# A sublayer's end: one feature quarter for all tokens, three quarters tile by tile

## The chip, the cores and the metric

The kernel runs on one core of one Trainium2 chip. The metric is the device time of one execution in microseconds; lower is better. The kernel before takes 3494.22 us, the median of three runs (3493.36 to 3494.25).

## The reference

One inference step of a small diffusion transformer: four layers, model width 1024, 128 context tokens and 512 latent tokens, all in 32-bit floats. Layer i mixes tokens by differential attention, neighbourhood attention, grouped-query attention or a long convolution ("hyena"), each followed by a squared-ReLU MLP of width 4096. Around each of the eight sublayers stands the same frame (xp is the context, xs the latent tokens):

```python
hp = modulate(xp, mod_p[0], mod_p[1])              # x * (1 + scale) + shift
...                                                # the mixer: op, os_ = ... @ w_o
xp = layer_norm(DN_ALPHA * xp + mod_p[2] * op, ln_g[i, 0], ln_b[i, 0])
xs = layer_norm(DN_ALPHA * xs + mod_s[2] * os_, ln_g[i, 0], ln_b[i, 0])
fp = squared_relu_mlp(modulate(xp, mod_p[3], mod_p[4]), mlp_w1[i], mlp_w2[i])
fs = squared_relu_mlp(modulate(xs, mod_s[3], mod_s[4]), mlp_w1[i], mlp_w2[i])
xp = layer_norm(DN_ALPHA * xp + mod_p[5] * fp, ln_g[i, 1], ln_b[i, 1])
xs = layer_norm(DN_ALPHA * xs + mod_s[5] * fs, ln_g[i, 1], ln_b[i, 1])
```

So a sublayer ends with a product (512 of the inner features at a time, here the last 512), its gated addition to the residual, a layer norm over the 1024 features of each token, and the modulation that begins the next sublayer.

## The kernel before

The 640 tokens are five tiles of 128 (`NT = 5`); tile 0 is the context. The residual `r` has tokens on the partitions. The input of a stage, `h`, has features on the partitions, since TensorE contracts over them. Every product is made of three (`mm3`, lines 473 to 475): each 32-bit operand is split into a rounded part and a rest (`hh` and `hl` for h, the two halves of a tile `hl...` for weights). A weight comes by DMA into one of three `raw` tiles; ScalarE casts it (line 450) and VectorE subtracts (line 451) into one of five `hl` tiles, in the order in which weights are wanted. `wget(key, ahead)` hands out a weight and has the conversion written for as many weights ahead.

A **group** is one tile's product with one feature **quarter** of 256 (`quarter`): 12 matmuls into one of four small PSUM banks. VectorE multiplies the result by the gate, which empties the bank into a tile `gtmp` (line 653), and the addition to `r` (line 660) is VectorE's if the group is `quick`, otherwise GpSimd's, but for one in four.

`sublayer_end` does the last 20 groups of a sublayer. Quarters 0 and 1 go over all five tiles; as soon as quarter 1 of a tile is added, the statistics of its first 512 features are taken (`ln_half`, line 682). Then, tile by tile, come quarters 2 and 3, both quick, and `ln_norm`: the second statistics, the aggregate, a square root on ScalarE (line 699), two small steps on VectorE, and the normalisation of the 1024 features on ScalarE (line 706; for the last tile half of it on VectorE, line 708).

`ln_out` turns a normalised tile into h: eight transposes on TensorE (line 736) into PSUM, scale and shift by ScalarE for four of the eight blocks (line 742) and by VectorE for the other four (line 745), casts to `hh` on ScalarE (line 746), and the rests into `hl` (line 748), on GpSimd for the first half of tiles 0, 2 and 3, on VectorE otherwise. In the end itself it is done for tiles 0 and 1 behind tile 3, and for tile 2 behind tile 4, with PSUM tiles of two banks of which there are two. Tiles 3 and 4 are left in `pending`: the next stage does its first products for tiles 0 and 1 (256 tokens, 24 matmuls a weight), then calls `flush` for tile 3, does the next weight's, and calls it for tile 4. The next stage's other 384 tokens come after that.

The order on VectorE, ScalarE and SyncE is set by a scheduler when the program is built; on GpSimd it is the written one, and on TensorE too from the `manual_schedule` in `sublayer_end` until the last tile is out. Each engine takes its instructions in that order. After it, `ln_residual` multiplies and shifts the residual by the layer norm's own gain and bias, on GpSimd and VectorE.

Seven of the eight sublayers end so; the last one takes the branch `if last`.

Of the kernel before, what the change touches and what calls it, by code (L numbers as in the profile page):

```python
# [24 lines left out]
NT = TOK // P  # L25
# [5 lines left out]
ALPHA = (2 * DEPTH) ** 0.25  # L31
# [247 lines left out]
class Trunk:  # L279
# [395 lines left out]
        self.hh = self.L(F32R, f"hh{self.tn}").rearrange("p (k t) -> p k t", k=KD)  # L675
        self.hl = self.L(F32R, f"hl_{self.tn}").rearrange("p (k t) -> p k t", k=KD)

    def ln_half(self, t, h, st=None):

        if st is None:  # L680
            st = self.small(12, "st").rearrange("p (a b) -> p a b", a=2)
        self.nc.vector.bn_stats(st[:, h], self.r[:, t, h * 512:(h + 1) * 512])  # L682
        return st

    def ln_norm(self, t, last=False):

        nc = self.nc
        r = self.r[:, t]
        if last:
            st = self.S(F32, "st", 24).rearrange("p (a b) -> p a b", a=4)  # L690
            for h in range(4):
                nc.vector.bn_stats(st[:, h], r[:, h * 256:(h + 1) * 256])
        else:
            st = self.st.pop(t) if t in self.st else self.ln_half(t, 0)
            self.ln_half(t, 1, st)
        mv = self.small(2, "mv")
        nc.vector.bn_aggr(mv, st)
        rs = self.small(2, "rs")
        nc.scalar.activation(rs[:, 0:1], mv[:, 1:2], AF.Sqrt, bias=self.eps[:, 0:1], scale=1.0)
        nc.vector.reciprocal(rs[:, 0:1], rs[:, 0:1])  # L700
        nc.vector.scalar_tensor_tensor(out=rs[:, 1:2], in0=mv[:, 0:1], scalar=-1.0, in1=rs[:, 0:1], op0=ALU.mult, op1=ALU.mult)
        if last:
            self.ln_last(r, rs)
            return
        cut = D if t < CT else 512
        nc.scalar.activation(r[:, 0:cut], r[:, 0:cut], AF.Identity, bias=rs[:, 1:2], scale=rs[:, 0:1])
        if cut < D:
            nc.vector.tensor_scalar(out=r[:, cut:], in0=r[:, cut:], scalar1=rs[:, 0:1], scalar2=rs[:, 1:2], op0=ALU.mult, op1=ALU.add)
# [73 lines left out]
    def sublayer_end(self, l, j, unit, group, last=False, spill=False, wide=False):  # L782


        if last:
            us = [unit(q, 1) for q in range(4)]
            for t in range(NT):
                for q in range(4):
                    group(us[q], t, q, t == NT - 1)
                self.ln_norm(t, t == NT - 1)  # L790
                if t < NT - 1:
                    self.ln_final(t)
            return
        self.modulation(l, j)
        self.new_h()
        self.st = {}
        for q in range(2):
            u = unit(q, 4)
            for t in range(NT):
                group(u, t, q, False)  # L800
                if q == 0 and self.ln_raw:
                    g = self.ln_raw.pop()
                    self.nc.scalar.mul(g, g, ALPHA)
                if q == 1:
                    self.st[t] = self.ln_half(t, 0)
        self.man.enter_context(self.tc.manual_schedule(engines={mybir.EngineType.PE, mybir.EngineType.Pool}))
        us = {2: unit(2, 4)}
        us[3] = unit(3, 3)
        for t in range(NT):
            for q in (2, 3):  # L810
                group(us[q], t, q, True)
            self.ln_norm(t)
            for i in {NT - 2: (0, 1), NT - 1: (2,)}.get(t, ()):
                self.ln_out(i, True)
        self.w_convert(self.wi + 4)
        self.pending = [lambda t=t: self.ln_out(t, wide) for t in range(3, NT)]
        self.after = self.spill if spill else self.ln_residual
# [1414 lines left out]
```

## Time and profile before

| | |
|---|---|
| median of three runs | 3494.22 us |
| the profiled execution | 3489.16 us |
| its span (first to last instruction) | 3487.3 us |
| TensorE busy | 3320.0 us, 95% |
| VectorE busy | 2584.9 us, 74% |
| ScalarE busy | 1510.8 us, 43% |
| GpSimd busy | 937.0 us, 27% |
| granted TensorE clock, mean | 0.983 |

Durations are of the one profiled execution. PE is TensorE, PEld its weight loads, DVE VectorE, ACT ScalarE, POOL GpSimd, SP SyncE. Busy times are averages over stages with different limits: what happens at a sublayer's end is read from the stretches around it, whose start is the span's start.

### The profile page before, as it was taken

Reading aid. Unit: us, or ns where it says so; the run is one execution under the profiler, and the core shown is the slowest. Engines: PE = TensorE matmul, PEld = TensorE weight load, DVE = VectorE, ACT = ScalarE, POOL = GpSimd, SP = SyncE. Lnnn points to the kernel's source line nnn. Section 1 sums busy time; section 2 is a strip of 40 time slices with the busy share of each in tenths; the row PEclk is TensorE's granted clock in tenths of the full one; section 3 lists DMA queues with packets and bytes.
Section 4 is the critical chain, followed back from the end, with each engine's and each line's share of the span. In section 5 each row is a group of like instructions: output and inputs, shape, how many; then the busy total and the mean of one; then the engine's idle time right before and its main releaser. Section 6 shows DMA issues by size and latency. Waiting matters only on the chain.

```text
span 3487.3 us, 63772 instructions
## 1 busy us (share of the span) xinstructions
PE 3320.0 (95%) x25288; PEld 3188.3 (91%) x25288; DVE 2584.9 (74%) x4806; ACT 1510.8 (43%) x2704; POOL 937.0 (27%) x912
## 2 busy tenths in 40 slices
PE   8999899999999999999998999999998999999998
PEld 6878898998999989999997889999997998999998
DVE  4776888788576678777677877787859888945457
ACT  4555453433366654333345665333325334432322
POOL 1332233334254433122232013232322112300002
PEclk9999999999999999999999999999999999999999
DMA  7333135545232324556422112545533224232221
GB/s 277 124 131 101 61 117 163 173 164 176 88 126 77 106 74 158 188 165 200 141 63 69 31 53 91 185 155 181 164 99 117 81 79 154 83 97 78 85 75 53
DMA packets 157643, 418.96 MB, mean 120 GB/s; under 512 B 19550, under 2 KB 29414, under 8 KB 154270
## 3 DMA queue, kind: packets, MB, share of 16 engines
q1 hardware_dynamic: 157344, 414.88, 36.3%
q8 instruction: 199, 3.26, 0.4%
q14 instruction: 100, 0.82, 0.1%
HBM read 371.20 MB, written 34.05 MB: 116 GB/s over the span
## 4 chain that ended last, share of the span: by engine, by line
PE 58%; DVE 13%; ACT 3%; issue 3%; POOL 1%; DMA 1%; SPq 0%; DVEq 0%; POOLq 0%; ACTq 0%
PE w L473 14%; PE w L474 14%; PE w L475 14%; DVE hl L451 2%; PE pv L2059 2%; DVE gtmp L653 2%; PE s L2012 1%; PE ptp L1062 1%; PE qk L474 1%; PE qk L475 1%; PE qk L473 1%; DVE ada L541 1%; DVE r L660 1%; PE py L1775 1%; DVE st L682 1%
## 5 line engine op out<-in xcount | busy, mean ns | idle before, releaser
L451 DVE TENSOR_TENSOR hl<-raw,hl 128x1024 fp32r<-128x1024 f32 x411 | 532.4, 1298 | 314.8 <-ACT hl L450 313.5
L450 ACT CAST hl<-raw 128x1024 fp32r<-128x1024 f32 x411 | 430.1, 1048 | 724.2 <-PE w L475 608.2
L473 PE MATMUL w<-hl,ff 128*128 128x256 f32 x2560 | 715.8, 280 | 7.7 <-DVE gtmp L653 7.5
L474 PE MATMUL w<-hl,ff 128*128 128x256 f32 x2560 | 715.3, 279 | 2.5 <-DVE hl L451 2.4
L475 PE MATMUL w<-hl,ff 128*128 128x256 f32 x2560 | 714.1, 279 | 0.0
L660 POOL TENSOR_TENSOR r<-r,gtmp 128x256 f32<-128x256 f32 x416 | 413.6, 1008 | 1106.0 <-DVE gtmp L653 1078.2
L473 PE MATMUL w<-hh,hl 128*128 128x320 f32 (+2 forms) x2048 | 639.7, 312 | 15.3 <-DVE h L745 9.3
L475 PE MATMUL w<-hh,hl 128*128 128x320 f32 (+2 forms) x2048 | 636.3, 311 | 0.0
L474 PE MATMUL w<-hl,hl 128*128 128x320 f32 (+2 forms) x2048 | 636.0, 311 | 0.0
L473 PEld LDWEIGHTS w<-hl,ff 128*128 128x128 f32 x2560 | 481.3, 188 | 12.7 <-DVE gtmp L653 10.7
L474 PEld LDWEIGHTS w<-hl,ff 128*128 128x128 f32 x2560 | 481.4, 188 | 4.9 <-DVE hl L451 3.3
L475 PEld LDWEIGHTS w<-hl,ff 128*128 128x128 f32 x2560 | 480.3, 188 | 0.0
L653 DVE TENSOR_TENSOR gtmp<-w,gate 128x256 f32<-128x256 f32 x800 | 326.9, 416 | 186.2 <-PE w L475 172.1
L541 DVE SCALAR_TENSOR_TENSOR ada<-adaw,sil,ada 128x512 f32<-128x512 f32 x504 | 387.6, 801 | 93.8 <-DMA adaw<-in_ada_w 82.9
L473 PEld LDWEIGHTS w<-hh,hl 128*128 128x128 f32 x2048 | 388.3, 190 | 30.4 <-issue 18.5
L475 PEld LDWEIGHTS w<-hh,hl 128*128 128x128 f32 x2048 | 388.5, 190 | 0.8 <-issue 0.8
L474 PEld LDWEIGHTS w<-hl,hl 128*128 128x128 f32 x2048 | 388.4, 190 | 0.3 <-issue 0.3
L886 ACT ACTIVATE fx<-w 128x640 f32<-128x640 f32 (+2 forms) x136 | 91.5, 673 | 464.5 <-PE w L475 451.1
L473 PE MATMUL qk<-hh,hl 128*128 128x320 f32 (+2 forms) x672 | 216.1, 322 | 4.0 <-ACT hh L746 3.7
L474 PE MATMUL qk<-hl,hl 128*128 128x320 f32 (+2 forms) x672 | 212.1, 316 | 2.2 <-DVE hl L748 2.2
L475 PE MATMUL qk<-hh,hl 128*128 128x320 f32 (+2 forms) x672 | 211.9, 315 | 0.6 <-DVE hl L451 0.6
L473 PE MATMUL w<-hl,oh 128*128 128x256 f32 x640 | 184.2, 288 | 10.1 <-DVE gtmp L653 5.5
(342 smaller groups left out, 6973.8 us busy)
## 6 DMA issues: line engine op xcount, KB each, us to landing
raw<-in_w SPq DMA_DIRECT2D x256, 512.0 KB
adaw<-in_ada_w SPq DMA_DIRECT2D x288, 256.0 KB
adaw<-in_ada_w SPq DMA_DIRECT2D x16, 1024.0 KB
raw<-ab_d SPq DMA_DIRECT2D x32, 512.0 KB
raw<-in_hy_in SPq DMA_DIRECT2D x24, 512.0 KB
adaw<-in_ada_s SPq DMA_DIRECT2D x8, 1024.0 KB
raw<-in_da_qk SPq DMA_DIRECT2D x16, 512.0 KB
gate<-gate_d SPq DMA_DIRECT2D x32, 256.0 KB
```

The source lines that it names most:

```text
L450: self.nc.scalar.copy(t[:, 0], raw)
L451: self.nc.vector.tensor_sub(t[:, 1], raw, t[:, 0].bitcast(F32))
L473: mm(ps, w[0], x[0], start=start, stop=False)
L474: mm(ps, w[0], x[1], start=False, stop=False)
L475: mm(ps, w[1], x[0], start=False, stop=stop)
L541: nc.vector.scalar_tensor_tensor(out=y, in0=raw[h], scalar=x, in1=y, op0=ALU.mult, op1=ALU.add)
L653: nc.vector.tensor_mul(tmp, ps, self.gate[2 * s + q // 2][:, (q % 2) * 256:(q % 2) * 256 + 256])
L660: eng.tensor_add(rv, rv, tmp)
L682: self.nc.vector.bn_stats(st[:, h], self.r[:, t, h * 512:(h + 1) * 512])
L886: nc.scalar.activation(x, src, AF.Relu)
L1062: nc.tensor.transpose(ps[:, i * P:(i + 1) * P], pr[:, (done + i) * P:(done + i + 1) * P], self.ident)
L2059: nc.tensor.matmul(ps[64 * h:64 * h + 64], self.v[:, self.chunk + c, vc:vc + 64], pts[h][:, c * P:(c + 1) * P], start=c == 0, stop=c == se ...
```

## The change

Quarter 0 alone goes over all five tiles. Then each tile gets quarters 1, 2 and 3 in a row (1 is not quick, 2 and 3 are), both statistics are taken in `ln_norm`, and from tile 2 on the transposes of the tile two places before follow. The three weights of quarters 1 to 3 are fetched together, with 4, 3 and 2 weights ahead instead of 4, 4 and 3. The written order for TensorE begins after quarter 0 instead of after quarter 1.

```diff
--- before.py
+++ after.py
@@ -675,13 +675,6 @@
         self.hh = self.L(F32R, f"hh{self.tn}").rearrange("p (k t) -> p k t", k=KD)
         self.hl = self.L(F32R, f"hl_{self.tn}").rearrange("p (k t) -> p k t", k=KD)
 
-    def ln_half(self, t, h, st=None):
-
-        if st is None:
-            st = self.small(12, "st").rearrange("p (a b) -> p a b", a=2)
-        self.nc.vector.bn_stats(st[:, h], self.r[:, t, h * 512:(h + 1) * 512])
-        return st
-
     def ln_norm(self, t, last=False):
 
         nc = self.nc
@@ -691,8 +684,9 @@
             for h in range(4):
                 nc.vector.bn_stats(st[:, h], r[:, h * 256:(h + 1) * 256])
         else:
-            st = self.st.pop(t) if t in self.st else self.ln_half(t, 0)
-            self.ln_half(t, 1, st)
+            st = self.small(12, "st").rearrange("p (a b) -> p a b", a=2)
+            for h in range(2):
+                nc.vector.bn_stats(st[:, h], r[:, h * 512:(h + 1) * 512])
         mv = self.small(2, "mv")
         nc.vector.bn_aggr(mv, st)
         rs = self.small(2, "rs")
@@ -793,25 +787,20 @@
             return
         self.modulation(l, j)
         self.new_h()
-        self.st = {}
-        for q in range(2):
-            u = unit(q, 4)
-            for t in range(NT):
-                group(u, t, q, False)
-                if q == 0 and self.ln_raw:
-                    g = self.ln_raw.pop()
-                    self.nc.scalar.mul(g, g, ALPHA)
-                if q == 1:
-                    self.st[t] = self.ln_half(t, 0)
+        u = unit(0, 4)
+        for t in range(NT):
+            group(u, t, 0, False)
+            if self.ln_raw:
+                g = self.ln_raw.pop()
+                self.nc.scalar.mul(g, g, ALPHA)
         self.man.enter_context(self.tc.manual_schedule(engines={mybir.EngineType.PE, mybir.EngineType.Pool}))
-        us = {2: unit(2, 4)}
-        us[3] = unit(3, 3)
+        us = {q: unit(q, 4 - max(0, q - 1)) for q in range(1, 4)}
         for t in range(NT):
-            for q in (2, 3):
-                group(us[q], t, q, True)
+            for q in range(1, 4):
+                group(us[q], t, q, q > 1)
             self.ln_norm(t)
-            for i in {NT - 2: (0, 1), NT - 1: (2,)}.get(t, ()):
-                self.ln_out(i, True)
+            if t > 1:
+                self.ln_out(t - 2, True)
         self.w_convert(self.wi + 4)
         self.pending = [lambda t=t: self.ln_out(t, wide) for t in range(3, NT)]
         self.after = self.spill if spill else self.ln_residual
```

On TensorE the eight transposes of tile 0 (tile `lnt`) stood with those of tile 1 behind the eighth group of the tile phase (tile 3), and now stand alone behind the ninth (tile 2); those of tile 1 stand behind tile 3, those of tile 2 behind tile 4 as before.

VectorE, first end, before: from tile 4's first multiply on (`gtmp609`, `gtmp611` are its quarters 2 and 3; `lnt602` and `lnt605` the transposes of tiles 0 and 1, `h32604` and `h32607` their second halves, `hl35` a weight, `st577` tile 4's statistics).

```order
L653 TENSOR_TENSOR gtmp609_4607<-w2608_4594,gate479_3718 128x256
L660 TENSOR_TENSOR r437_3495<-r437_3495,gtmp609_4607 128x256
L653 TENSOR_TENSOR gtmp611_4623<-w2610_4610,gate479_3718 128x256
L745 TENSOR_SCALAR h32604_4564<-lnt602_4548,gs_77,bs_78 128x128 x4
L660 TENSOR_TENSOR r437_3495<-r437_3495,gtmp611_4623 128x256
L451 TENSOR_TENSOR hl35_4658<-raw35_4200,hl35_4658 128x1024
L748 TENSOR_TENSOR hl_552_4190<-h32604_4564,hh552_4189 128x4x128
L745 TENSOR_SCALAR h32607_4587<-lnt605_4571,gs_77,bs_78 128x128 x3
L748 TENSOR_TENSOR hl_552_4190<-h32606_4580,hh552_4189 128x4x128
L745 TENSOR_SCALAR h32607_4587<-lnt605_4571,gs_77,bs_78 128x128
L682 BN_STATS st577_4379<-r437_3495 128x6
```

The two tiles' evacuations, a weight conversion and tile 4's additions stand in one row there. After, from tile 3's quarter 1 on (`gtmp594`; `gtmp596` and `gtmp598` are its quarters 2 and 3, `lnt590` and `h32592` are tile 0's, `st599` is tile 3's statistics):

```order
L653 TENSOR_TENSOR gtmp594_4503<-w2593_4490,gate439_3503 128x256
L695 SCALAR_TENSOR_TENSOR rs589_4462<-mv588_4460,rs589_4462 128x1
L739 TENSOR_SCALAR h32592_4483<-lnt590_4467,gs_77,bs_78 128x128 x4
L653 TENSOR_TENSOR gtmp596_4519<-w2595_4506,gate479_3718 128x256
L689 BN_STATS st599_4538<-r437_3495 128x6
L742 TENSOR_TENSOR hl_552_4190<-h32592_4483,hh552_4189 128x4x128
L660 TENSOR_TENSOR r437_3495<-r437_3495,gtmp596_4519 128x256
L653 TENSOR_TENSOR gtmp598_4535<-w2597_4522,gate479_3718 128x256
L660 TENSOR_TENSOR r437_3495<-r437_3495,gtmp598_4535 128x256
L689 BN_STATS st599_4538<-r437_3495 128x6
```

Tile 0's evacuation now lies among tile 3's groups, and tile 3's first statistics, which read what GpSimd added, stand before its last multiply. Tile 1's last subtractions (`h32603`, `h32604`) and tile 4's groups (`gtmp606` to `gtmp610`) follow:

```order
L742 TENSOR_TENSOR hl_552_4190<-h32603_4557,hh552_4189 128x4x128
L653 TENSOR_TENSOR gtmp606_4584<-w2605_4571,gate439_3503 128x256
L653 TENSOR_TENSOR gtmp608_4600<-w2607_4587,gate479_3718 128x256
L653 TENSOR_TENSOR gtmp610_4616<-w2609_4603,gate479_3718 128x256
L660 TENSOR_TENSOR r437_3495<-r437_3495,gtmp608_4600 128x256
L660 TENSOR_TENSOR r437_3495<-r437_3495,gtmp610_4616 128x256
L689 BN_STATS st611_4619<-r437_3495 128x6
L742 TENSOR_TENSOR hl_552_4190<-h32604_4564,hh552_4189 128x4x128
L689 BN_STATS st611_4619<-r437_3495 128x6
```

The weight conversion that stood between has gone behind them.

GpSimd, first end, before: the end of its additions (`gtmp564` to `gtmp576` are quarter 1's) and the subtractions of the first halves of tiles 0, 2 and 3.

```order
L660 TENSOR_TENSOR r437_3495<-r437_3495,gtmp564_4304 128x256
L660 TENSOR_TENSOR r437_3495<-r437_3495,gtmp567_4322 128x256
L660 TENSOR_TENSOR r437_3495<-r437_3495,gtmp573_4358 128x256
L660 TENSOR_TENSOR r437_3495<-r437_3495,gtmp576_4376 128x256
L748 TENSOR_TENSOR hl_552_4190<-h32603_4557,hh552_4189 128x4x128
L748 TENSOR_TENSOR hl_552_4190<-h32615_4644,hh552_4189 128x4x128
L748 TENSOR_TENSOR hl_552_4190<-h32620_4703,hh552_4189 128x4x128
```

All four additions stood before the first subtraction. After, the same work:

```order
L660 TENSOR_TENSOR r437_3495<-r437_3495,gtmp564_4306 128x256
L660 TENSOR_TENSOR r437_3495<-r437_3495,gtmp573_4364 128x256
L742 TENSOR_TENSOR hl_552_4190<-h32591_4476,hh552_4189 128x4x128
L660 TENSOR_TENSOR r437_3495<-r437_3495,gtmp594_4503 128x256
L660 TENSOR_TENSOR r437_3495<-r437_3495,gtmp606_4584 128x256
L742 TENSOR_TENSOR hl_552_4190<-h32615_4639,hh552_4189 128x4x128
L742 TENSOR_TENSOR hl_552_4190<-h32620_4703,hh552_4189 128x4x128
```

Tile 0's subtraction (`h32591`) now stands between the additions of quarter 1 for tiles 1 and 3 (tile 2's is VectorE's), and those of tiles 3 and 4 stand behind it.

## Rows read from the trace of the kernel before

**Rows 1.** the page, busy time, share of the span and instructions of TensorE
```profile
PE 3320.0 (95%) x25288; PEld 3188.3 (91%) x25288; DVE 2584.9 (74%) x4806; ACT 1510.8 (43%) x2704; POOL 937.0 (27%) x912
```

**Rows 2.** windows, seven sublayer ends: length, engines' busy us (instructions), PEclk, DMA
```profile
435.66:452.32 16.66, 10.47 (x74) 9.86 (x73) 14.56 (x40) 14.25 (x27) 4.38 (x2) 0.80 0.09 32
...
1283.46:1300.98 17.52, 12.06 (x75) 11.28 (x73) 14.98 (x40) 14.26 (x27) 4.39 (x2) 0.72 0.13 35
...
sum 115.30, PE 77.56 PEld 72.37 DVE 102.36 ACT 94.86 POOL 27.65; mean PE 11.08 PEld 10.34 DVE 14.62 ACT 13.55 POOL 3.95
```

**Rows 3.** timeline, TensorE, first end: start, us, instruction, count, [idle before <- releaser]
```profile
437.40 1.09 PE L736 MATMUL lnt<-ident,r 128*128 128x128 f32 x8 [0.71 <-ACT r L706]
...
443.30 1.06 PE L736 MATMUL lnt<-ident,r 128*128 128x128 f32 x8 [2.08 <-ACT hh L746]
447.77 0.55 PE L473 MATMUL w<-hh,hl 128*128 128x256 f32 x1 [3.41 <-DVE h L745]
...
448.33 0.41 PE L475 MATMUL w<-hh,hl 128*128 128x256 f32 x1
448.55 0.41 PE L473 MATMUL w<-hh,hl 128*128 128x256 f32 x1
```

**Rows 4.** windows, stretches of the first end
```profile
424.40:435.66 11.26, 11.26 (x97) 11.26 (x97) 9.18 (x24) 4.06 (x5) 1.44 (x2) 1.00 0.16 47
435.66:447.77 12.11, 5.92 (x50) 5.31 (x49) 10.02 (x29) 11.38 (x22) 3.09 (x1) 0.87 0.12 45
...
458.00:478.00 20.00, 19.36 (x123) 18.78 (x122) 19.24 (x17) 13.43 (x24) 14.87 (x10) 1.00 0.00 1
...
417.32:461.76 44.44, 38.25 (x312) 37.64 (x311) 36.33 (x84) 27.07 (x50) 14.15 (x12) 0.92 0.18 62
```

**Rows 5.** timeline, VectorE, first end
```profile
428.74 0.75 DVE L653 TENSOR_TENSOR gtmp<-w,gate 128x256 f32<-128x256 f32 x2
429.40 0.75 DVE L660 TENSOR_TENSOR r<-r,gtmp 128x256 f32<-128x256 f32 x2
430.19 0.69 DVE L682 BATCH_NORM_STATS2 st<-r 128x6 f32<-128x512 f32 x1
...
441.79 1.37 DVE L745 TENSOR_SCALAR h<-lnt,gs,bs 128x128 f32<-128x128 f32 x4
...
443.40 1.22 DVE L451 TENSOR_TENSOR hl<-raw,hl 128x1024 fp32r<-128x1024 f32 x1
444.54 0.69 DVE L748 TENSOR_TENSOR hl<-h,hh 128x512 fp32r<-128x512 f32 x1
```

**Rows 6.** timeline, ScalarE, first end
```profile
437.26 0.28 ACT L699 ACTIVATE rs<-mv,epst 128x1 f32<-128x1 f32 x1
...
438.16 1.24 ACT L706 ACTIVATE r<-r,rs 128x1024 f32<-128x1024 f32 x1 [0.28 <-DVE rs L701]
...
441.65 1.03 ACT L450 CAST hl<-raw 128x1024 fp32r<-128x1024 f32 x1
...
446.46 1.52 ACT L742 ACTIVATE h<-lnt,bs,gs 128x128 f32<-128x128 f32 x4
```

**Rows 7.** timeline, GpSimd, first end
```profile
443.28 3.09 POOL L748 TENSOR_TENSOR hl<-h,hh 128x512 fp32r<-128x512 f32 x1 [16.31 <-ACT hh L746]
449.08 1.29 POOL L748 TENSOR_TENSOR hl<-h,hh 128x512 fp32r<-128x512 f32 x1 [2.71 <-ACT hh L746]
```

**Rows 8.** line 660 on GpSimd: count, ns min/median/max, first and last start
```profile
L660 POOL TENSOR_TENSOR r<-r,gtmp x416: 717/742/1735, 414.9 to 2995.4; 128x256 f32<-128x256 f32 x139
```

**Rows 9.** timeline, TensorE, in the third and the fourth mixer
```profile
1837.72 2.50 PE L1392 MATMUL rk<-ident,rk 128*128 128x128 f32 x10 [5.02 <-ACT rk L1389]
...
2661.01 0.93 PE L1722 MATMUL ztp<-ident,x 128*128 128x128 f32 x2 [4.45 <-DVE x L1687]
```

**Rows 10.** windows, from tile 0's transposes to those waits
```profile
2621.62:2664.00 42.38, 30.47 (x202) 28.28 (x200) 39.41 (x75) 22.49 (x49) 20.03 (x13) 0.91 0.23 88
1792.24:1837.00 44.76, 34.98 (x258) 33.87 (x256) 41.57 (x85) 27.13 (x54) 19.45 (x13) 0.96 0.14 40
```

## The prediction

> **What bounds the kernel now.** I read the page first: TensorE has work in 95% of the span [rows 1], so the change can only win where TensorE stands still or runs slowly. Then the busy times by stretch, at the seven places where a sublayer ends by this code (the eighth end takes the other branch, which is untouched). Each stretch runs from the first transpose of tile 0 to the first transpose of tile 3, by which time TensorE has done three tiles' transposes (8 x some 0.13 = 1.03 us each), tile 4's two groups and the next stage's first unit, 24 matmuls each. A group of 12 takes 1.41 us: 8 groups fill the 11.26 us before the first transposes [rows 4]. So the work is 3 x 1.03 + 4 x 1.41 = 8.7 us, and the seven stretches take 115.3 us [rows 2], where 7 x 8.7 = 61 would do. **54 us, 7.7 us per end, is all that this change can win**, 1.5% of the span.
>
> The timeline of TensorE at the first end says what the 7.7 us are [rows 3]: it waits 0.71 us before tile 1's transposes, 2.08 before tile 2's (for a place in PSUM), 3.41 before the next stage's first product, 6.2 in all; and then 24 products take 4.55 us, from 447.77 [rows 3] to the stretch's end at 452.32 [rows 2], where 2.82 would do. The granted clock of the first stretch is 0.80 on the mean, and 0.72 in the longest of the seven [rows 2], and after the waits consecutive products start 0.22 us apart [rows 3] where the phase before them has 0.117 (11.26 us over 96): part of them ran at 1.2 instead of 2.4 GHz.
>
> Who is late: between 435.66 and 447.77 VectorE is busy 10.02 of 12.11 us and ScalarE 11.38 [rows 4]. Two tiles' transposes come at once, a third soon after, and the evacuations, two normalisations and two weight conversions queue on both engines. From the start of quarter 1 to the last evacuation VectorE has 36.33 us of work in 44.44 [rows 4], so 8.1 us of it were idle, mostly early, while it waited for products.
>
> **The change part by part.** Removed: nothing of TensorE's work; the statistics of the first half, taken early in quarter 1, become part of the tile's own step. Added: nothing. Moved: quarter 1's five groups go between quarters 0 and 2 of each tile, so a tile takes 3 x 1.41 = 4.23 us instead of 2.82; tile 0's transposes stand behind tile 2, tile 1's behind tile 3, tile 2's behind tile 4; and the third and fourth of the next stage's weights are converted late. I walk the first end with zero at quarter 0's first product (18 groups = 25.4 us before 435.66, so 410.27).
>
> TensorE alone: tile 0's transposes at 14 x 1.41 = 19.7 (before 25.4), tile 1's at 25.0, tile 2's at 30.3, the next stage at 31.3 (before 37.5), its first unit done at 34.1 (before 42.05).
>
> VectorE, by the new order and its rows: per group 0.375 to empty PSUM and, for quarters 2 and 3, 0.375 to add [rows 5]; per tile two statistics of 0.69 [rows 5] and, as an estimate, as much as half of one in small steps. That is 3 x 0.375 + 2 x 0.375 + 2.5 x 0.69 = 3.6 us in a tile of 4.23, so it keeps pace through tiles 0 to 2. Tile 0 is normalised at 17.3 (last addition 12.6, statistics 13.2, ScalarE's root 0.28 and 1.24 [rows 6], behind TensorE's pace at each step), 2.4 us before its transposes: the first wait is gone. With a tile's evacuation on top (1.37 for four, 0.69 for the subtraction [rows 5]) VectorE needs 5.7 us for tiles 3 and 4, where TensorE needs 4.23 + 1.03 = 5.26: it falls behind by 0.4 us a tile.
>
> The added wait: tile 3's quarter-1 addition stands on GpSimd behind tile 0's subtraction, which needs ScalarE's copy of that tile (four steps of 1.52 together from 20.4 [rows 6], a root between them, a cast: 22.9). VectorE reaches tile 3's first statistics at 24.4 and waits for that addition. With 1.29 for the subtraction [rows 7] and 0.74 for the addition [rows 8] it is there by some 25.3, with 3.09, the longest subtraction [rows 7], by 27. Queued behind the waiting instruction are the multiplies that empty PSUM for tiles 3 and 4; TensorE can run four groups ahead on the four small banks, 5.6 us, so it does not feel 1 to 2.6 us. What does feel it is tile 1's evacuation, last in that queue: ScalarE's casts follow two weight conversions (1.03 each [rows 6]), which wait for tile 4's groups to free their buffers at 27.4 and 28.9, and a normalisation; the second cast ends at 32.7, VectorE's subtraction at 33.8, with the long GpSimd time at 35.5. The next stage's first half unit (1.41 us from 31.3) runs without it, the second half waits 1.1, or 2.9 in all in the long case.
>
> Which of the two? The long row of 3.09 [rows 7] lies beside VectorE's weight conversion and subtraction at 443.40 and 444.54 [rows 5]; the next one took 1.29. The Trainium skill (SBUF — State Buffer, "SBUF: two separate sides") says that VectorE with two inputs from SBUF and GpSimd lock each other out of a shared port pair for a whole instruction. The trace agrees (3.09 against 1.29); by that rule the short case holds, since in the new order VectorE runs evacuations from PSUM there, and the sum below would be 5 x 5.7 + 2 x 3.3 = 35 us; by the long row it would be 5 x 3.9 + 2 x 3.3 = 26. Leaving the rule aside I take the middle, 2.0 us of waiting left per end, since all seven ends have that pattern and nothing shows how it falls at each.
>
> Clock: with waits of 1 to 3 us left, some ends will still drop to 1.2 GHz. A drop here costs 1.7 us in the first end (4.55 - 2.82); I take half of it, 0.9.
>
> So an end is left with 2.9 of its 7.7 us and saves 4.8. For two ends the saving cannot stay whole. In the third mixer TensorE next waits 5.02 us before 1837.72, in the fourth 4.45 us before 2661.01 [rows 9], and up to there VectorE is busy 41.57 of 44.76 and 39.41 of 42.38 us [rows 10]: only its idle time, 3.2 and 3.0 us there plus what it idles in quarter 1, can be cut, and some remains. I take 3.3 for each. Sum: 5 x 4.8 + 2 x 3.3 = **31 us**.
>
> Conversions: two fall into the crowded place before, three now (the third weight's goes from 17 to 37); the third and fourth weights are wanted 2 x (2.82 + 1.03) = 7.7 us and more after the next stage begins and are there some 2 us before. Their buffers free the raw tiles later, so SyncE's queue holds the following weight loads some 19 us longer (37.3 instead of 18.5); these are wanted near 68, when the next stage's second round of units begins. I cost both at nothing; if the cover were gone, a few tenths per end.
>
> The profiled execution took 3489.16 us (span 3487.3 and 1.9 around it), 5.06 under the median of the runs, 3494.22. 3489.2 - 31 = 3458; with the 5 us, **3463 us**.
>
> **The rivals.** (a) Given back: VectorE, not TensorE, is the chain at all seven ends, as it is saturated for the 20 us after (19.24 of 20.00 in 458 to 478 [rows 4]). Then only cut idle time counts, some 2.4 of its 8.1 us by the walk with the long GpSimd times: 17 us, 3477. For it: ScalarE and VectorE are both full; against: behind five ends TensorE waits little in the 40 us that follow, and the 20 us are mostly residual work that nobody waits for soon. (b) Nothing of the waits is left, and the clock stays up: 7 x 6.5 = 46 us, 3448. For it: tile 1 has 5.3 us of cover after its transposes and its evacuation alone is 2 us; against: ScalarE's queue as walked. (c) The waits only move: tile 4 normalises late (38.9 in the walk, transposes due at 39), so the first unit's gain is lost before tile 4's transposes: 3494. Against it: ScalarE would have to be 5 us later than walked. (d) Slower: GpSimd holds VectorE. If each of tiles 3 and 4 waits for a subtraction of 3.09 and an addition of 1.73, the longest of that line [rows 7, 8], VectorE is 3.3 us late per tile, 6.6 in all; that passes the 5.6 us that TensorE can run ahead, from where each us counts, and the stop brings 1.7 us of slow clock: 1.1 + 6.6 + 1.7 = 9.4 us left per end against 7.7, +12 us, 3506. Against it: between the two GpSimd additions there is a tile's time.
>
> **How the numbers follow.** Forecast (24 to 40 us won) 0.55, (a) 0.22, (b) 0.07, (c) 0.09, (d) 0.07. Around 3494 a change under 7 us, 0.2%, cannot be told from none. Faster: 0.55 + 0.22 + 0.07 = 0.84; same: 0.09; slower: 0.07. The range runs from (b), 3448, to past (a), 3484, which leaves out (c) and (d), 16 in 100.
>
> **What would show it.** Right: in the seven stretches from tile 0's first transpose to tile 3's, which now hold six groups of tiles 3 and 4 and come to 14.4 us of work each, the excess falls from 54 to some 20 us; waits before transposes vanish; the first product waits mostly for tile 1's second half, VectorE's statistics on GpSimd's addition 1 to 2.6 us per end; fewer drops to 1.2 GHz there. (a) shows as longer waits on VectorE within 40 us after; (d) as matmuls waiting for gtmp inside the tile phase. The forecast is wrong if tile 4's normalisation ends more than 5 us later than walked, or if VectorE meets waits that the walk lacks.

## The result and the profile after

The changed kernel takes **3451.23 us** (median of four runs, 3449.80 to 3454.18), the kernel before 3493.79 beside it (3491.28 to 3494.25): ratio 0.9881, 95% interval 0.9864 to 0.9898, some 42.6 us won. The forecast was 3463, with 31 won. The 42.6 lie above the likeliest case's 24 to 40 us; the time is inside the range, which reached down to rival (b), 3448. The profiled execution took 3451.18 us (span 3449.3, mean granted clock 0.991), so the two traces differ by 38.0 us of span; the remaining 4.6 come from the profiled execution of before, which was a short one.

The page of the changed kernel, busy times:

```profile
PE 3303.5 (96%) x25288; PEld 3172.8 (92%) x25288; DVE 2573.7 (75%) x4806; ACT 1513.0 (44%) x2704; POOL 961.5 (28%) x912
```

Against [rows 1]: TensorE's busy time falls by 16.5 us with the same 25288 instructions, so that much was products at the slower clock; the other 21.5 us of the span were standing still (167.3 before, 145.8 now, span less busy).

The windows of the changed kernel, the seven ends from tile 0's first transpose to tile 3's (columns as in [rows 2]: length, PE, PEld, DVE, ACT, POOL, PEclk, DMA):

```profile
428.98:444.27 15.29, 14.41 (x123) 14.02 (x121) 13.81 (x39) 13.56 (x25) 2.75 (x3) 1.00 0.01 2
...
2588.73:2604.43 15.70, 14.64 (x122) 14.11 (x121) 14.22 (x41) 13.39 (x25) 3.30 (x4) 1.00 0.19 68
...
sum 107.60, PE 101.01 PEld 98.14 DVE 97.24 ACT 94.31 POOL 20.28; mean PE 14.43 PEld 14.02 DVE 13.89 ACT 13.47 POOL 2.90
```

The stretch holds 14.4 us of work now and takes 15.4. Of the 54 us of excess, 107.6 - 7 x 14.4 = 6.8 are left: 47 us were won inside the ends. The granted clock is 1.00 at all seven, where it was 0.72 to 0.89 (two of them in [rows 2]). TensorE's own timeline at the first end:

```profile
428.98 1.03 PE L730 MATMUL lnt<-ident,r 128*128 128x128 f32 x8
...
434.10 1.03 PE L730 MATMUL lnt<-ident,r 128*128 128x128 f32 x8
...
439.22 1.03 PE L730 MATMUL lnt<-ident,r 128*128 128x128 f32 x8
440.01 0.37 PE L473 MATMUL w<-hh,hl 128*128 128x256 f32 x1
...
442.89 0.39 PE L474 MATMUL w<-hl,hl 128*128 128x256 f32 x1 [0.79 <-DVE hl L742]
```

The three waits of [rows 3] (0.71, 2.08, 3.41) are gone, the three sets of transposes stand 5.12 us apart, and the next stage's first product follows at once. What is left is one wait of 0.79 in the middle of the first unit, for VectorE's rest of tile 1's second half. VectorE at that place (start, us, instruction):

```profile
434.64 0.69 DVE L689 BATCH_NORM_STATS2 st<-r 128x6 f32<-128x512 f32 x1 [0.92 <-POOL r L660]
...
439.77 1.08 DVE L653 TENSOR_TENSOR gtmp<-w,gate 128x256 f32<-128x256 f32 x3
440.77 0.86 DVE L660 TENSOR_TENSOR r<-r,gtmp 128x256 f32<-128x256 f32 x2
441.56 0.68 DVE L689 BATCH_NORM_STATS2 st<-r 128x6 f32<-128x512 f32 x1
442.16 0.67 DVE L742 TENSOR_TENSOR hl<-h,hh 128x512 fp32r<-128x512 f32 x1
```

And GpSimd, beside [rows 7]:

```profile
432.61 1.31 POOL L742 TENSOR_TENSOR hl<-h,hh 128x512 fp32r<-128x512 f32 x1 [8.89 <-ACT hh L740]
433.88 0.73 POOL L660 TENSOR_TENSOR r<-r,gtmp 128x256 f32<-128x256 f32 x1
440.27 0.75 POOL L660 TENSOR_TENSOR r<-r,gtmp 128x256 f32<-128x256 f32 x1 [5.66 <-DVE gtmp L653]
```

VectorE waits 0.92 us for GpSimd's addition of tile 3, and then has no pause up to the subtraction that TensorE waits for. GpSimd's own subtraction took 1.31, not 3.09.

What was not won lies outside the ends. TensorE stood still 167.3 - 37.7 = 129.6 us outside them before (the 37.7 is 115.30 - 77.56 in [rows 2]), and 145.8 - 6.6 = 139.2 now: **9.6 us are given back**. Of these, 1.3 stand ahead of the first end's quarter 0, where the two executions run the same work, so some 8.3 can be the change's. Two waits that grew, TensorE in the third and the fourth mixer of the changed kernel, beside [rows 9]:

```profile
1817.67 0.80 PE L1381 MATMUL rk<-ident,rk 128*128 128x128 f32 x2 [6.01 <-ACT rk L1378]
...
2619.03 0.44 PE L474 MATMUL hyin<-hl,hl 128*128 128x384 f32 x1 [3.24 <-DVE hl L742]
```

The first was 5.02 [rows 9]. The second is new at that size (0.7 at the longest before). Behind it the wait of 4.45 [rows 9] has become 0.41; the next one, 2.29 before, is 2.44.

### The profile page after: what moved, and what is told of

It is laid out like the page before. It is cut to its first block, busy times and chain, and to the rows that moved or that the text cites. A ratio compares the mean times of both kernels' runs of the same rounds, so it can differ in the third digit from the quotient of the medians.

```text
span 3449.3 us, 63752 instructions
## 1 busy us (share of the span) xinstructions
PE 3303.5 (96%) x25288; PEld 3172.8 (92%) x25288; DVE 2573.7 (75%) x4806; ACT 1513.0 (44%) x2704; POOL 961.5 (28%) x912
## 4 chain that ended last, share of the span: by engine, by line
PE 53%; DVE 14%; issue 5%; DMA 3%; ACT 2%; POOL 1%; SPq 0%; DVEq 0%; POOLq 0%; ACTq 0%
PE w L473 12%; PE w L474 12%; PE w L475 12%; DVE hl L451 2%; DVE ada L541 2%; DMA adaw<-in_ada_w 2%; PE pv L2048 2%; DVE gtmp L653 2%; PE s L2001 1%; PE ptp L1051 1%; PE qk L473 1%; PE qk L475 1%; PE qk L474 1%; DVE r L660 1%; PE py L1764 1%
## 5 line engine op out<-in xcount | busy, mean ns | idle before, releaser
L451 DVE TENSOR_TENSOR hl<-raw,hl 128x1024 fp32r<-128x1024 f32 x411 | 540.4, 1317 | 322.7 <-ACT hl L450 321.4
L473 PEld LDWEIGHTS w<-hh,hl 128*128 128x128 f32 x2048 | 384.1, 188 | 17.9 <-issue 8.4
L475 PEld LDWEIGHTS w<-hh,hl 128*128 128x128 f32 x2048 | 384.2, 188 | 0.8 <-issue 0.8
```

Source lines behind the costliest of these rows:

```text
L451: self.nc.vector.tensor_sub(t[:, 1], raw, t[:, 0].bitcast(F32))
L473: mm(ps, w[0], x[0], start=start, stop=False)
L475: mm(ps, w[1], x[0], start=False, stop=stop)
```

## The experiments

Each was timed beside the kernel before. Medians are given with the range of their runs.

**1. The transposes alone.** The old order of quarters, each tile's transposes behind the tile two places on:

```diff
-            for i in {NT - 2: (0, 1), NT - 1: (2,)}.get(t, ()):
-                self.ln_out(i, True)
+            if t > 1:
+                self.ln_out(t - 2, True)
```

> The kernel before with one part of the change: tile 0's transposes behind tile 2, tile 1's behind tile 3, tile 2's behind tile 4; quarters 0 and 1 still go over all tiles first. Theory 'spread' (a tile's evacuation has to get a tile step of its own, and the step has to be long enough): tile 0 is normalised some 2 us after its transposes are due, so a new wait of about 2 us stands before them, and a part of the first product's wait goes; 1 to 2.5 us saved per end, 3477 to 3488. Rival 'order of the transposes alone': all of the gain is here, about 3451. Rival 'order of the products alone': nothing changes, 3494.

Measured: 3473.82 us (3472.94 to 3476.05), ratio 0.9945 [0.9928, 0.9961]: 19 us won, a little more than expected. TensorE at the first end, and the windows of the first and the fourth end (tile 0's to tile 3's transposes):

```profile
434.03 0.33 PE L736 MATMUL lnt<-ident,r 128*128 128x128 f32 x1 [2.62 <-ACT r L706]
```

```profile
434.03:448.48 14.45, 13.43 (x96) 12.86 (x97) 11.36 (x34) 12.44 (x25) 1.37 (x1) 0.88 0.00 1
...
1784.02:1798.32 14.30, 12.05 (x97) 11.24 (x97) 13.19 (x38) 13.28 (x26) 1.87 (x2) 1.00 0.06 18
```

With two quarters per tile, tile 0 is not normalised when its transposes are due: a wait of 2.62 takes the place of the later ones, and the clock falls (0.88). At the fourth end that wait is 1.05 and the clock stays.

**2. The order of the products alone.** The changed kernel with the old place of the transposes:

```diff
-            if t > 1:
-                self.ln_out(t - 2, True)
+            for i in {NT - 2: (0, 1), NT - 1: (2,)}.get(t, ()):
+                self.ln_out(i, True)
```

> The changed kernel with the old places of the transposes: tiles 0 and 1 together behind tile 3, tile 2 behind tile 4; the products stay in the new order. Theory 'spread': both normalisations are done in time, so the waits before tile 1's transposes go, but two evacuations come at once again: first product some 2 to 3 us late, clock drops at some ends; 3 to 4 us saved per end, 3466 to 3473. Rival 'order of the products alone': 3451. Rival 'order of the transposes alone': 3494.

Measured: 3477.87 us (3473.78 to 3483.86), ratio 0.9956 [0.9940, 0.9971]: 15 us won, less than expected. The first end's first product, and the windows of the first and the third end:

```profile
446.81 0.36 PE L473 MATMUL w<-hh,hl 128*128 128x256 f32 x1 [3.18 <-DVE h L739]
```

```profile
436.60:450.94 14.34, 11.16 (x86) 10.95 (x85) 13.45 (x33) 13.17 (x25) 3.94 (x3) 0.90 0.01 2
...
1282.57:1295.76 13.19, 9.94 (x87) 9.73 (x86) 12.39 (x32) 12.37 (x24) 3.94 (x3) 1.00 0.01 1
```

Now the waits before the transposes are gone and the long one before the first product stays, 3.18 against 3.41 [rows 3]: two tiles' evacuations still come at once. 19 and 15 make 34, both together 42.6: each part takes away waits that the other leaves, and neither is the whole. Experiment 2 also has the late conversions of the change (experiment 7); experiment 1 has not.

**3. All four quarters tile by tile.**

```diff
-        u = unit(0, 4)
-        for t in range(NT):
-            group(u, t, 0, False)
...
-        us = {q: unit(q, 4 - max(0, q - 1)) for q in range(1, 4)}
+        us = {q: unit(q, 4 - q) for q in range(4)}
         for t in range(NT):
-            for q in range(1, 4):
+            for q in range(4):
```

The written order for TensorE and GpSimd then begins ahead of quarter 0.

> The changed kernel with all four quarters tile by tile (a tile step of 5.64 us), transposes as in the changed kernel; weights fetched 4, 3, 2, 1 ahead. Theory 'spread': tile 1's evacuation gets 1.4 us more cover, the remaining 0.85 us per end before its second half goes, some 6 us less than the changed kernel, 3445. Rival 'weights': only the first of the next stage's weights is converted before tile 4's groups, the second is wanted 3.9 us into the next stage and comes late, 2 to 3 us more per end than the changed kernel, 3465 to 3472.

Measured: 3451.42 us (3449.08 to 3454.03), ratio 0.9879 [0.9864, 0.9893], the same time as the changed kernel: neither expectation. The window of its first end, and TensorE behind it:

```profile
428.44:445.21 16.77, 16.77 (x147) 16.77 (x146) 15.13 (x38) 12.71 (x24) 4.63 (x5) 1.00 0.01 1
```

```profile
459.57 0.44 PE L474 MATMUL w<-hl,hl 128*128 128x384 f32 x1 [1.50 <-DVE hl L742]
```

The end itself is without a gap (16.77 busy of 16.77), and the 0.8 us saved there come back as a wait of 1.50 for the last evacuation, some 14 us on (1.45 to 1.50 at four of the seven ends).

**4. Quarter 1's additions on VectorE.**

```diff
-                group(us[q], t, q, q > 1)
+                group(us[q], t, q, True)
```

> The changed kernel with quarter 1's additions on VectorE too, so that its statistics no longer wait for GpSimd (0.92 us of VectorE's time at the first end) and four more additions of 0.375 fall on it per end. Theory 'ScalarE's queue holds the last evacuation': the first product's second half waits as long as now or up to 0.5 us longer, 3451 to 3455. Rival 'GpSimd's addition is on the path': the wait of 0.85 us per end goes, 3445.

Measured: 3458.18 us (3456.39 to 3464.13), ratio 0.9901 [0.9886, 0.9916]: some 7 us slower than the changed kernel, and slower than either expectation. TensorE behind the first end:

```profile
448.54 0.33 PE L730 MATMUL lnt<-ident,r 128*128 128x128 f32 x1 [1.01 <-ACT r L700]
...
460.46 0.69 PE L474 MATMUL w<-hl,hl 128*128 128x384 f32 x1 [2.19 <-DVE hl L742]
```

VectorE no longer waits for GpSimd, but has the additions itself; tile 4 is normalised late, and its evacuation too. So waiting 0.92 us for GpSimd costs VectorE less than doing these additions itself.

**5 and 6. Less for VectorE behind the ends.** Both kernels without the layer norm's gain and bias on features 512 to 1023 of the residual:

```diff
-        for h, eng in ((0, self.nc.gpsimd), (1, self.nc.vector)):
+        for h, eng in ((0, self.nc.gpsimd),):
```

> The changed kernel, with the layer norm's gain and bias left out of the residual for features 512 to 1023, which is VectorE's half of ln_tile (some 93 us of VectorE in all, 13 us behind each end). Theory 'VectorE takes back': the 47 us won inside the seven ends are worth only 42 because VectorE is full for the 20 to 40 us behind each end; freed of 13 us there, the changed kernel keeps them, and it stands 46 to 50 us below the old kernel with the same part left out. Rival 'something else': the 5 us go to other waits (GpSimd's part, loads, the clock behind), and the two differ by 39 to 43 us as before. Its own time: 3430 to 3446 by the first, 3445 to 3452 by the rival.

> The old kernel with the same part left out (VectorE's half of the residual's gain and bias). Its own waits stand mostly ahead of that work, so both theories give a small gain, 3480 to 3493; what tells them apart is its distance to the changed kernel with the same omission: 46 to 50 us if VectorE takes gains back behind the ends, 39 to 43 if not.

Measured: the changed kernel so takes 3435.07 us (3431.06 to 3437.37), the kernel before 3481.00 (3477.37 to 3483.51): 45.9 apart, on the edge of the first theory. The changed kernel's page and the sum of its seven ends; then the same of the kernel before:

```profile
PE 3298.5 (96%) x25288; PEld 3168.9 (92%) x25288; DVE 2504.7 (73%) x4736; ACT 1510.9 (44%) x2704; POOL 944.4 (28%) x912
```

```profile
sum 106.87, PE 100.63 PEld 98.04 DVE 96.60 ACT 93.71 POOL 20.24; mean PE 14.38 PEld 14.01 DVE 13.80 ACT 13.39 POOL 2.89
```

```profile
PE 3318.5 (95%) x25288; PEld 3187.6 (92%) x25288; DVE 2517.0 (72%) x4736; ACT 1511.9 (43%) x2704; POOL 934.5 (27%) x912
```

```profile
sum 114.75, PE 77.59 PEld 72.49 DVE 102.14 ACT 93.60 POOL 27.61; mean PE 11.08 PEld 10.36 DVE 14.59 ACT 13.37 POOL 3.94
```

With spans of 3433.3 and 3479.2, TensorE stands still 134.8 and 160.7 us, of it 6.2 and 37.2 in the ends and 128.6 and 123.5 outside: 5.1 us are given back in place of 9.6. Ahead of the first end's quarter 0, where the omission has done nothing yet, these two executions differ by 0.6 the other way, so behind it 8.3 have become 5.7. A part of the give-back hangs on VectorE's residual work behind the ends, a third to a half by these single executions; the share is not settled. The wait of 6.01 in the third mixer becomes 0.51 without that work, but the one of 3.24 in the fourth stays (experiment 5):

```profile
2609.04 0.63 PE L474 MATMUL hyin<-hl,hl 128*128 128x384 f32 x1 [3.24 <-DVE hl L742]
```

It is a wait for the last evacuation, which VectorE finishes late. Another 3 us of the difference between the two kernels lie in TensorE's busy time outside the ends: 3318.5 - 77.6 = 3240.9, of which 7 x 5.7 = 39.9 are work that the changed kernel has inside its stretches, leaves 3201.0, against 3197.9. The runs' times alone, 42.6 and 45.9 apart with ranges of 4 to 6 us, would not settle it.

**7. The late conversions alone.** The kernel before with one weight fewer ahead for quarters 2 and 3:

```diff
-        us = {2: unit(2, 4)}
-        us[3] = unit(3, 3)
+        us = {2: unit(2, 3)}
+        us[3] = unit(3, 2)
```

> The old kernel with only the number of weights converted ahead changed (4, 4, 3, 2 in place of 4, 4, 4, 3). Theory: the late conversions by themselves neither help nor hurt, 3490 to 3497. Rival: they crowd the end, where VectorE and ScalarE are full, and cost 1 us at each of seven ends: 3500; then part of what the change could win is lost to them. Other rival: they free VectorE early in quarter 1 and are worth a part of the 42 us: under 3487.

Measured: 3486.50 us (3483.57 to 3495.74, 11 runs), ratio 0.9986 [0.9976, 0.9996]. TensorE's waits at its first end, in us:

```profile
PE w L473 <- DVE h L745: 3.5, 1, 3.5
PE lnt L736 <- DVE h L745: 1.1, 1, 1.1
```

Crowding is out. The interval allows 1 to 8 us of gain: of the three waits of [rows 3], the long one stays, 0.71 and 2.08 have become 1.1. But the profiled execution took 3492.19 us, no less than that of before; it is one of the four long ones of the eleven (3492.19 to 3495.74, the other seven 3483.57 to 3486.91). So that some of the 42.6 us are the conversions' is likely and not shown.

**8. Fewer weights asked for at the very end.**

```diff
-        self.w_convert(self.wi + 4)
+        self.w_convert(self.wi + 2)
```

> The changed kernel, with only two weights in place of four asked for ahead at the end of the sublayer (the rest follow when the next stage asks). Theory: the 0.8 us that the next stage's first unit still waits for tile 1's second half is ScalarE's and VectorE's work behind tile 4, weight conversions among it; with these later the wait goes and 3 to 6 us are won, 3445 to 3448. Rival: the scheduler places the casts as early as before, or the wait moves on to tile 4's evacuation or to the weights: 3449 to 3456.

Measured: 3461.24 us (3459.43 to 3470.20), ratio 0.9913 [0.9899, 0.9927]: 10 us slower than the changed kernel, more than the rival said. TensorE behind its first end:

```profile
464.76 0.44 PE L474 MATMUL w<-hl,hl 128*128 128x384 f32 x1 [1.46 <-DVE hl L742]
```

And VectorE there, then VectorE of the changed kernel at its last evacuation:

```profile
455.75 1.62 DVE L451 TENSOR_TENSOR hl<-raw,hl 128x1024 fp32r<-128x1024 f32 x1
457.29 1.79 DVE L742 TENSOR_TENSOR hl<-h,hh 128x512 fp32r<-128x512 f32 x1
...
461.02 1.99 DVE L451 TENSOR_TENSOR hl<-raw,hl 128x1024 fp32r<-128x1024 f32 x1
462.94 1.76 DVE L742 TENSOR_TENSOR hl<-h,hh 128x512 fp32r<-128x512 f32 x1
```

```profile
451.71 1.28 DVE L742 TENSOR_TENSOR hl<-h,hh 128x512 fp32r<-128x512 f32 x2
452.91 1.22 DVE L451 TENSOR_TENSOR hl<-raw,hl 128x1024 fp32r<-128x1024 f32 x1
454.05 0.68 DVE L742 TENSOR_TENSOR hl<-h,hh 128x512 fp32r<-128x512 f32 x1
```

GpSimd beside them, on the residual, first here and then in the changed kernel:

```profile
456.24 2.28 POOL L748 TENSOR_TENSOR r<-r,ln_g 128x512 f32<-128x512 f32 x1
```

```profile
451.75 7.16 POOL L749 TENSOR_TENSOR r<-r,ln_b 128x512 f32<-128x512 f32 x1
```

The 0.8 us in the first unit stays at six of seven ends. The last subtraction starts 8.5 us behind tile 4's transposes (454.45) in place of 6.0 (448.01). The same two conversions and two subtractions stand ahead of it in both kernels, but they take 6.2 us here and 3.7 in the changed kernel. Here VectorE's instructions and GpSimd's lengthen each other in turn; there VectorE runs on, and GpSimd's addition, begun 0.04 us behind it, takes 7.16 us. So, by these rows, the changed kernel has its last evacuation in time at four of its seven ends (GpSimd's additions of 7.15 to 12.98 us) because VectorE shuts GpSimd out there. Nothing in the change aims at that. In experiments 3, 8 and 9 the two take turns at these ends, the last subtraction starts 7.5 to 9.1 us behind tile 4's transposes, and TensorE waits for it. No run moves GpSimd's residual work alone, so what that would win is untested. The profiled execution took 3470.20 us, the longest of the five, and 6.5 us of its distance to the changed kernel's lie ahead of the first end (tile 0's transposes at 435.44 against 428.98).

**9. Tile 1's first subtraction on GpSimd.**

```diff
-            sub = nc.gpsimd.tensor_sub if h == 0 and t in (0, 2, 3) else nc.vector.tensor_sub
+            sub = nc.gpsimd.tensor_sub if h == 0 and t < 4 else nc.vector.tensor_sub
```

> The changed kernel, with tile 1's first-half subtraction (into hl) given to GpSimd instead of VectorE. In the changed kernel GpSimd idles 5.66 us before tile 4's quarter-1 addition at 440.27, and the operands of that subtraction are there at 439.06, so it fits. Theory 'VectorE's queue': the 0.85 us that the next stage's first unit waits for tile 1's second half at each of seven ends is VectorE's queue, in which this 0.68 us stands ahead; it shrinks to 0.2 to 0.5 and 2 to 5 us are won, 3446 to 3449. Rival 'GpSimd holds' (the slower case of the prediction, here made likelier): tile 4's addition comes late behind it, VectorE's statistics wait, and the ends lengthen by 1 us or more: 3456 or more. Rival 'ScalarE': the wait is for the cast before it and nothing changes, 3450 to 3453.

Measured: 3456.22 us (3451.51 to 3458.04), ratio 0.9892 [0.9878, 0.9905]: 5 us over the changed kernel by the medians, with ranges that overlap. VectorE, GpSimd and TensorE at its first end:

```profile
439.33 1.68 DVE L451 TENSOR_TENSOR hl<-raw,hl 128x1024 fp32r<-128x1024 f32 x1
...
442.14 0.68 DVE L742 TENSOR_TENSOR hl<-h,hh 128x512 fp32r<-128x512 f32 x1
```

```profile
438.62 1.30 POOL L742 TENSOR_TENSOR hl<-h,hh 128x512 fp32r<-128x512 f32 x1 [4.52 <-ACT hh L740]
439.87 1.73 POOL L660 TENSOR_TENSOR r<-r,gtmp 128x256 f32<-128x256 f32 x1
```

```profile
442.88 0.39 PE L474 MATMUL w<-hl,hl 128*128 128x256 f32 x1 [1.24 <-DVE hl L742]
```

None of the three theories holds as put. The place that came free on VectorE went to a weight conversion, which took 1.68, and GpSimd's addition beside it took 1.73. The awaited subtraction starts 13.64 us behind tile 0's transposes (428.50) in place of 13.18, and the wait is 1.24, with 1.22 to 1.25 at the other ends.

**10. Tile 4's too** (the condition is `h == 0` alone).

> As the run before, and tile 4's first-half subtraction on GpSimd too. Theory: tile 4's evacuation becomes VectorE's 0.7 us shorter, but GpSimd's 1.3 us (up to 3.1 beside VectorE) delays the next stage's second unit of tokens: 3446 to 3452. Rival: GpSimd and VectorE slow each other down there and it costs 1 us per end against the run before.

Measured: 3464.53 us (3462.23 to 3469.26), ratio 0.9919 [0.9906, 0.9933]: 8 us over experiment 9, which is the rival's price. That the two engines slow each other more is not shown: TensorE's waits in the ends are nearly those of experiment 9, and most of the loss lies in the stretches between the ends. A wait that grew is in the fourth mixer, TensorE (3.03 in experiment 9, 0.41 in the changed kernel):

```profile
2640.92 0.93 PE L1711 MATMUL ztp<-ident,x 128*128 128x128 f32 x2 [6.57 <-DVE x L1676]
```

**11. Experiment 3 with the edit of experiment 10.**

> All four quarters tile by tile, with the first-half subtractions of all five tiles on GpSimd. In the run with four quarters alone the ends had no waits, but tile 4's evacuation was 1.5 us late at the first end and nothing was won. Theory: with 1.4 us less on VectorE in its queue that wait goes, 3442 to 3447. Rival: the wait only moves to GpSimd's subtraction or to the mixer behind, 3449 to 3454.

Measured: 3461.78 us (3460.57 to 3468.40), ratio 0.9913 [0.9899, 0.9926]: worse than experiment 3 by 10 us, and worse than its rival said. Tile 4's wait behind the first end is gone, and others have come; TensorE's waits behind the second end:

```profile
PE qk L475 <- DVE hl L451: 4.5, 1, 4.5
```

Here it is a weight that is converted late; the same wait is 0.9 in experiment 3. Of all the versions that do the whole work none beats the changed kernel; experiment 3 equals it.

## Why the prediction was right, and which sizes were not

*TensorE's walk* held within 0.6 us. From the zero of the walk, here 428.98 - 19.7 = 409.3, tile 1's transposes stand at 24.8 (walked 25.0), tile 2's at 29.9 (30.3), the next stage's first product at 30.7 (31.3).

*The added wait* held in its place and, by its short case, in its size. VectorE reached tile 3's statistics at 24.4 (walked 24.4), the addition was there at 25.3 (25.3), the awaited subtraction ended at 33.5 (33.8). TensorE waited 0.79 for it, 0.85 or so at the other ends, where the short case gave 1.1.

*Which case:* I had put 2.0 us, the middle of 1.1 and 2.9, although the reason for the short one was on the table. GpSimd's subtraction of 1.31 lay beside VectorE's four evacuations at 432.03, which read PSUM. The Trainium skill (SBUF — State Buffer, "SBUF: two separate sides") says that a GpSimd instruction and a VectorE instruction with two SBUF inputs shut each other out. The trace agrees on both sides (1.31 there; 1.73 in experiment 9, beside the conversion of 1.68). By that rule alone the sum was 35.

*The clock term* was mis-sized: 0.9 us per end, measured none. I argued that with 1 to 3 us left some ends would drop. The granted clock stayed at 1.00 in all seven stretches, with waits of 0.79 to 0.86, and in experiment 9 too, with 1.22 to 1.25. Longer waits came with either: in experiment 1 it is 0.88 to 0.89 at the four ends with a first wait of 2.17 to 2.62 and 1.00 at the three with one of 1.05 or 1.06; in experiment 2 it is 0.90 at the first end, after 3.18, and 1.00 at the third, after 3.25. The length of the wait alone does not tell.

So the term "an end is left with 2.9 of its 7.7 us" should have been 1.0 (6.8 over seven ends), and an end saves 6.7, not 4.8: 47 us in place of 7 x 4.8 = 34.

*What is given back* was too small in the prediction and put in two places only: 2 x 1.5 = 3 us, measured 9.6. The two mixers themselves were right: 3.3 forecast for each, 3.5 and 3.2 by the traces (what the end saved, less what the stretch up to the next end lost). But the stretches behind the first three ends, the first two MLPs and the second mixer, lost 1.5 to 2.8 us each as well. In the first MLP and the second mixer it is mostly waits for what VectorE makes, longer by 1 us and less each (`hab` and `gtmp`; `m`, `oh` and `hl`); in the second MLP TensorE hardly waits more, and the cause is open. The stretch ahead of the first end, the same in both kernels, differs by 1.0. That is rival (a) in part: its mechanism holds for a third to a half of the give-back (experiments 5 and 6), and its price, 17 us won in place of 31, was far off, since most of VectorE's late work has no one waiting for it. 47 - 9.6 = 37.6 is the 38.0 of the traces.

The two errors pull against each other, 13 us too little won inside the ends and 6.6 too little given back. That the sum, 31, missed the 38.0 of the traces by only 7 is partly luck.

*The other rivals.* (b) was the nearest in time, 3448, for another reason than it said: it had 46 us won with nothing given back. (c), tile 4 normalised late, happens where VectorE gets more work (experiment 4, waits of 0.83 to 1.39 before tile 4's transposes at six of the seven ends) and, by 0.45 to 0.89, in experiment 11; (d), GpSimd holding VectorE, is the 0.92 us at 434.64, of which TensorE feels nothing during the tiles.

*Conversions and loads* cost nothing, as forecast. ScalarE waits longer for weight loads; TensorE does not wait longer for the converted weights. ScalarE's waits for `in_w` and TensorE's for converted weights, before and then after (us, times, longest):

```profile
PE w L474 <- DVE hl L451: 2.4, 2, 1.3
...
ACT hl L450 <- DMA raw<-in_w: 4.8, 3, 2.2
```

```profile
PE w L474 <- DVE hl L451: 2.5, 3, 1.3
...
ACT hl L450 <- DMA raw<-in_w: 18.9, 7, 6.0
```

What stays open: the rest of the give-back, beyond the late evacuation in the fourth mixer, and how much of the gain the later conversions make by themselves.

## What to carry to other kernels

Where two engines hand a tile back and forth, leave the matmul engine as much work between a tile's last product and its next use as the hand-over takes, one tile at a time: bunching two tiles' evacuations (experiment 2) left about as much to win as normalising too late (experiment 1), and each edit alone won less than half. Once the waits at such a place are down to one short one, look at the sum of work behind it: here no further relief (experiments 3, 4, 8, 9, 10, 11) won anything. The wait grew, or another came at a later evacuation or conversion; VectorE is busy 18.63 of the 20 us behind the changed kernel's first end, and which of VectorE and GpSimd holds out the other there changed with the order. An instruction moved off a scheduled engine leaves a place that the scheduler fills, so compare the new order before counting the gain.

## What the runs showed of the hardware

A VectorE instruction with two inputs from SBUF and a GpSimd instruction lengthen each other, and in these rows the one that began second paid. At the first end of the kernel before, VectorE's addition was running when GpSimd's subtraction began at 443.28, and the conversion and VectorE's subtraction followed without a break until 445.23 [rows 5]:

```profile
443.07 0.42 DVE L660 TENSOR_TENSOR r<-r,gtmp 128x256 f32<-128x256 f32 x1
```

GpSimd's subtraction took 3.09 in place of 1.29 [rows 7] and ended 1.14 us behind VectorE's. In the changed kernel GpSimd's began first, by 0.23 us: it took 1.30, and the conversion 2.14 in place of 1.22. In experiment 9 the conversion began inside GpSimd's subtraction and took 1.68, and GpSimd's addition, begun inside the conversion, took 1.73 in place of 0.75. VectorE's instructions in an unbroken row keep GpSimd out for all of them: GpSimd's addition at 451.75 (experiment 8) ended 7.16 us later, 1.16 behind the last of VectorE's row, which ran from 451.71 to 457.75. The rows of the changed kernel, GpSimd and VectorE:

```profile
444.59 1.30 POOL L742 TENSOR_TENSOR hl<-h,hh 128x512 fp32r<-128x512 f32 x1 [3.57 <-ACT hh L740]
```

```profile
444.82 2.14 DVE L451 TENSOR_TENSOR hl<-raw,hl 128x1024 fp32r<-128x1024 f32 x1
```
